# The recurrence of an RWKV-7 and pooling block on one core: a longer planned gap for the triangular inverse, the next pair but one begun earlier, and one table for exp and ln

## The chip, the core and the metric

The kernel runs on one core of a Trainium2 chip. A core has a matrix engine (TensorE, PE in the profile, with its weight loads as PEld), VectorE (DVE), ScalarE (ACT), GpSimd (POOL) and SyncE (SP), which here issues nearly all DMAs, in order, on one queue. Each engine runs its own instructions in a fixed order and waits on semaphores for the others. The metric is the device time of one execution in microseconds, the median of several; lower is better.

## The reference

One block of a decoder with 512 tokens and width 2048, in float32. A combined projection of the normalised input feeds two mixers: RWKV-7 heads (16 heads of 64) and causal pooling over windows of 2, 4, 8 and 16 tokens; then an output projection and a gated MLP with a short convolution.

```python
def _wkv7_scan(r, w, k, v, a, b):
    def step(S, inp):
        r_t, w_t, k_t, v_t, a_t, b_t = inp
        sa = jnp.einsum('bhvk,bhk->bhv', S, a_t)
        S = S * w_t[:, :, None, :] + sa[..., None] * b_t[:, :, None, :] + v_t[..., None] * k_t[:, :, None, :]
        y = jnp.einsum('bhvk,bhk->bhv', S, r_t)
        return S, y

def reference(x, c, ...):
    mod = c_act @ w_ada[l] + b_ada[l]
    h = _rmsnorm(x, norm1_g[l]) * (1.0 + sc1) + sh1
    p = h @ w_in[l]
    y_rwkv = _rwkv7_mixer(p[..., :N_RWKV_COLS], ...)
    y_pool = _pool_mixer(p[..., N_RWKV_COLS:], ...)
    x = x + gt1 * (jnp.concatenate([y_rwkv, y_pool], axis=-1) @ w_out[l])
    h = _rmsnorm(x, norm2_g[l]) * (1.0 + sc2) + sh2
    x = x + gt2 * _conv_ffn(h, w_up[l], conv_w[l], conv_b[l], w_down[l])
    return _rmsnorm(x, norm_f_g)
```

## The kernel before

**Stages.** The first 160 us stream adaLN weights and the first part of the input projection. The last stage, from 859 us on, is the output projection and the MLP. Between them lies the stretch that the change touches, the function `recurrence`, which interleaves four things on PE.

- *The rest of the input projection*: 27 output tiles of 128 columns, each 16 steps deep; each step is three matmuls of 512 columns (`mm3`, L122 to L124), since every float32 operand is split into a high and a low part. ACT casts the high part of the weights (`whi`, L115), DVE subtracts the low part (`wlo`, L117). `units` yields after each step, so three matmuls go together. Finished tiles are shifted and spilled to DRAM (`spill`, `sp`).
- *Part a of a head pair* (`stage_a`): decay and gate factors from small matmuls and sigmoids (L404 to L410), a scan, two exponentials (`ep`, `em`), the norm of k by ln and exp (`inv`, L432 to L434), then `ar` and `bt`. `scores` (L381) makes the 64x64 triangular matrices of eight chunks and two heads, masked into `sb` (L447).
- *The inverse of their 16x16 diagonal blocks*: the blocks go through DRAM (`dn`) into `nl`, one block per partition; 28 small DVE steps (L464 to L473) solve them; the result `xyl` goes through DRAM (`dxz`) into `x4w`, and ACT copies it to `x4` (L483).
- *Part b* (`stage_b`): scores of the other keys, four transposes into token rows (L502, copied by ACT, L503), from L530 on the 16-blocks are joined to 32 and 64 with small matmuls, then the chunk products, six scan steps over chunks (L601 on PE, L602 on DVE in turn), the output, and a normalisation and gate (L614 to L629).

Beside these, pool groups (L300) and the adaLN products (`ada_rest`, `war`, 192 tiles of 256 KB multiplied on DVE at L354) are spread over the stretch.

**What sets the order.** PE's order is written by hand: `recurrence` keeps a clock of planned microseconds. Each generator yields a pair (PE time of the step just issued, planned wait until its next step); the loop issues the first ready step of part b, part a or a pool group, and where none is ready a step of the projection. The inverse is planned as 27 us after the scores (`q.inverted`). A pair's part a starts when its projections are `made` and the pair two before has `left` its output. The order on ACT, DVE and SP isn't by hand: the scheduler of the framework sets it from priorities and its own estimate of times, and tiles with few buffers (`pa`: two PSUM banks; `ring`: seven; `x4c`, `ep`, `em`: one) hold a writer back until the readers are done.

```python
q.inverted = clock[0] + 27.0
...
if live["a"] is None and na < NP and na in made and (na < 2 or hasattr(qs[na - 2], "left")):
    live["a"], ready["a"] = stage_a(na, qs[na]), clock[0]
...
for c in "bap":
    if live[c] is not None and ready[c] <= clock[0]:
        break
```

Of the kernel before, what the change touches and what calls it, by code (L numbers as in the profile page):

```python
# [9 lines left out]
F32 = mybir.dt.float32  # L10
# [47 lines left out]
def block_kernel(ctx, tc, a, out, stop=None, dbg=None):  # L58
# [211 lines left out]
    def load_pw(gi):  # L270
        t = ra.tile([P, T], F32, tag="war", name="pw", bufs=3) if gi < 3 else ring("pw")
# [66 lines left out]
    dxz = [tc.dram_tile([32, 2, 32, 32], F32, name=f"dxz{i}") for i in range(2)]  # L338
    for i in range(2):
        nc.sync.dma_start(dxz[i][:, :, :, :].rearrange("l w i j -> (l w i j)").rearrange("(p n) -> p n", p=P),  # L340
                          x4w[:, :, :, 0:32])

# [29 lines left out]
    class Pair:  # L372
        pass
# [10 lines left out]
    def stage_a(p, q):  # L384
# [10 lines left out]
        lw = q.lw = ra.tile([P, 3, P], F32, tag="lw", name="lw", bufs=2)  # L395
        nc.sync.dma_start(lw, a["lora"][p, :, :, :])
# [7 lines left out]
        PE.matmul(psw, lw[0:64, 0, :], xwa[0:64, :], start=True, stop=True)  # L404
        PE.matmul(psal, lw[64:128, 0, :], xwa[64:128, :], start=True, stop=True)
# [4 lines left out]
        S.activation(al, psal, AF.Sigmoid, bias=col("a0", p))  # L410
        cs = ra.tile([P, NL, L + 1], F32, tag="sg", name="cs", bufs=2)
# [12 lines left out]
        yield 1.4, 2.0  # L424
# [4 lines left out]
        ar = q.ar = ra.tile([P, 2, NL, L], F32, tag="ar", name="ar", bufs=2)  # L429
        V.tensor_mul(ar[:, 1, :, :], ch(r), ep[:, :, 1 : L + 1])  # L430
# [5 lines left out]
        V.scalar_tensor_tensor(ar[:, 0, :, :], ch(inv), -1.0, ep[:, :, 0:L], op0=ALU.mult, op1=ALU.mult)  # L436
# [3 lines left out]
        yield 0.9, 13.0  # L440
# [9 lines left out]
        dn = tc.dram_tile([32, 32, 32], F32, name=f"dn{p}")  # L450
        for b in range(4):
            nc.sync.dma_start(dn[8 * b : 8 * b + 8, :, :].rearrange("s i j -> i s j"), nt[BS[b], :, half32(b)])
        nl = ra.tile([64, 16, 16], F32, tag="nl", name="nl")
        for e in range(2):
            es = slice(16 * e, 16 * e + 16)
            nc.sync.dma_start(nl[32 * e : 32 * e + 32, :, :], dn[0:32, es, es])
# [17 lines left out]
        dx = dxz[p % 2]  # L474
        for e in range(2):
            es = slice(16 * e, 16 * e + 16)
            for w in range(2):
                nc.sync.dma_start(dx[:, w, es, es], xyl[32 * e : 32 * e + 32, w, :, :])
        for b in range(4):
            nc.sync.dma_start(x4w[BS[b], :, :, half32(b)],  # L480
# [3 lines left out]
        q.inverted = clock[0] + 27.0  # L484
        yield 1.4, 6.0
# [19 lines left out]
    def stage_b(p, q):  # L505

        sb, x4, ar, bt, kt, v, fdec = q.sb, q.x4, q.ar, q.bt, q.kt, q.v, q.fdec
        nt = sb[:, :, 0, :]
# [10 lines left out]
        yield 1.4, 0.0  # L519
        to_rows(lambda c: v[:, c * P : (c + 1) * P], by_head(tok[:, 0, :, :]))  # L520
        to_rows(lambda c: ar[:, 0, 2 * c : 2 * c + 2, :].rearrange("p e t -> p (e t)"), by_head(rw[:, :, 0, :]))
        yield 0.9, 1.0
        to_rows(lambda c: bt[:, c * P : (c + 1) * P], by_head(sb[:, :, 2, :]))
        to_rows(lambda c: kt[:, c * P : (c + 1) * P], by_head(tok[:, 1, :, :]))
        yield 0.9, max(1.5, q.inverted - clock[0] - 0.9)
# [11 lines left out]
        yield 2.1, 1.6  # L537
# [6 lines left out]
        yield 2.1, 2.3  # L544
# [8 lines left out]
        yield 1.2, 1.6  # L553
# [3 lines left out]
        yield 1.2, 1.6  # L557
# [8 lines left out]
        yield 2.1, 1.6  # L566


        lo, hi = slice(0, NC * L), slice(NC * L, 2 * NC * L)
        first = {"start": False, "skip_group_check": True}  # L570
        pg = btile()
        for c, e, h, j, s in items:
            PE.matmul(pg[HS[h], e, jl(c)], rw[HS[e], s, 0, :], sb[HS[e], s, 2, :], start=c == 0, stop=True,
                      skip_group_check=True)
        for c, e, h, j, s in items:
            PE.matmul(pg[HS[h], e, jl(NC + c)], sb[HS[e], s, 2, :], rw[HS[e], s, 1, :], stop=False, **first)
        for c, e, h, j, s in items:
            PE.matmul(pg[HS[h], e, jl(NC + c)], tok[HS[e], 1, s, :], tok[HS[e], 0, s, :], stop=True, **first)
        py = btile("py")
        for c, e, h, j, s in items:  # L580
            PE.matmul(py[HS[h], e, jl(c)], rw[HS[e], s, 0, :], sb[HS[e], s, 1, :], start=c == 0, stop=True,
                      skip_group_check=True)
        for h in range(2):
            V.tensor_tensor(gd[HS[h], :, HS[h]].rearrange("p (c e) k -> p e c k", e=2),
                            pg[HS[h], :, lo].rearrange("p e (c k) -> p e c k", c=NC),
                            ident[HS[h], None, None, HS[h]].to_broadcast([64, 2, NC, L]), op=ALU.add)
        hs = rw[:, :, 0, :]
        V.tensor_tensor(hs.rearrange("p (c e) d -> p e c d", e=2), pg[:, :, hi].rearrange("p e (c d) -> p e c d", c=NC),
                        fdec[:, :, :].rearrange("p (c e) o -> p e c o", e=2).to_broadcast([P, 2, NC, L]), op=ALU.mult)
        for c, e, h, j, s in items:  # L590
            PE.matmul(py[HS[h], e, jl(NC + c)], rw[HS[e], s, 1, :], sb[HS[e], s, 1, :], stop=False, **first)
        for c, e, h, j, s in items:
            PE.matmul(py[HS[h], e, jl(NC + c)], tok[HS[e], 0, s, :], sk[HS[e], s, 1, :], stop=j == 0, **first)
# [739 lines left out]
```

## Time and profile before

| | us |
|---|---|
| median of 3 runs (lowest to highest) | 2441.68 (2439.91 to 2449.15) |
| the profiled execution | 2447.94 |
| its span, first to last instruction | 2446.0 |

PE is busy for 2217.8 us of the span (91%), PEld 1972.2, DVE 1620.6, ACT 1049.9. The mean granted TensorE clock is 0.964 of full speed.

How to read the rows that the prediction shows. A row of stretches gives the window and its length, then the busy time and number of instructions of PE, PEld, DVE, ACT and POOL, the granted clock, the share of the DMA engines and GB/s. A row of waits gives who waited for whom, the total in us, the number of times and the longest. A row in order of time gives start, length, engine, line, operation and tiles, and in brackets the idle time before it with what ended it; matmuls overlap, so the cost of one is the distance between starts. A row of groups has the count, the busy time, the mean in ns, and the idle time before them. A float32 matmul of the small kind stands as two rows of PE.

### The profile page before, as it was taken

What the parts mean: (1) busy time and instruction counts of PE and PEld (TensorE: products, weight loads), DVE (VectorE), ACT (ScalarE), POOL (GpSimd) and SP (SyncE); (2) the same over time, 40 slices, a digit from 0 to 9 for tenths busy, and PEclk for the clock granted to TensorE, in tenths of its full rate; (3) what the DMA queues carried; (4) which work ended last, traced back from release to release, by engine and by line L of the source; (5) the groups of instructions that cost most, each with busy time, mean ns of one, the idle gap of its engine ahead of it and who ended that gap; (6) DMA issues with size and microseconds to landing.
All of it is one profiled execution on the core that took longest, in us unless ns stands there. A gap on an engine that the chain in (4) does not pass through costs nothing.

```text
span 2446.0 us, 43166 instructions
## 1 busy us (share of the span) xinstructions
PE 2217.8 (91%) x17346; PEld 1972.2 (81%) x17346; DVE 1620.6 (66%) x2543; ACT 1049.9 (43%) x1447; POOL 126.3 (5%) x183
## 2 busy tenths in 40 slices
PE   4766866867888999999999999999999999999997
PEld 3645655655666779999999999999999988888897
DVE  7987776765446445678888887777777735353354
ACT  3232422424334334665555555555555622233353
POOL 0000000000000001001011010000000000110000
PEclk9988988889999999999999999999999999999998
DMA  9978667653433275669888887777777757764464
GB/s 352 336 229 231 184 196 205 188 152 101 96 77 77 80 249 184 182 212 261 241 240 237 237 233 199 198 200 201 196 197 194 256 166 277 255 195 129 112 182 162
DMA packets 226235, 482.89 MB, mean 197 GB/s; under 512 B 74545, under 2 KB 79729, under 8 KB 217841
## 3 DMA queue, kind: packets, MB, share of 16 engines
q1 hardware_dynamic: 206114, 413.01, 52.6%
q0 software_dynamic: 18864, 66.07, 13.2%
q8 instruction: 136, 2.23, 0.4%
q10 hardware_dynamic: 1056, 1.05, 0.1%
q14 instruction: 65, 0.53, 0.1%
HBM read 441.50 MB, written 38.54 MB: 196 GB/s over the span
## 4 chain that ended last, share of the span: by engine, by line
PE 48%; issue 8%; DVE 1%; DMA 1%; ACT 0%; POOL 0%; POOLq 0%; DVEq 0%; ACTq 0%
PE b L124 16%; PE b L123 16%; PE b L122 16%; DMA wrow<-wup 1%; DVE ulo L923 0%; DVE xr L851 0%; ACT x L854 0%; DVE t L977 0%; POOL x L1207 0%; ACT t L859 0%; ACT uhi L921 0%; DVE u L952 0%; DVE wlo L117 0%; DVE t L963 0%; DVE t L969 0%
## 5 line engine op out<-in xcount | busy, mean ns | idle before, releaser
L124 PE MATMUL b<-t,ulo 128*128 128x256 f32 x1408 | 397.2, 282 | 0.0
L122 PE MATMUL b<-t,uhi 128*128 128x256 f32 x1408 | 396.8, 282 | 0.0
L123 PE MATMUL b<-t,uhi 128*128 128x256 f32 x1408 | 396.7, 282 | 0.0
L124 PE MATMUL b<-act,ulo 128*128 128x512 f32 (+1 forms) x880 | 308.0, 350 | 0.0
L123 PE MATMUL b<-act,uhi 128*128 128x512 f32 (+1 forms) x880 | 307.8, 350 | 0.0
L122 PE MATMUL b<-act,uhi 128*128 128x512 f32 (+1 forms) x880 | 307.7, 350 | 0.0
L122 PE MATMUL b<-y,uhi 128*128 128x256 f32 x1056 | 297.4, 282 | 2.3 <-ACT uhi L921 2.3
L124 PE MATMUL b<-y,ulo 128*128 128x256 f32 x1056 | 297.3, 282 | 0.7 <-DVE ulo L923 0.6
L123 PE MATMUL b<-y,uhi 128*128 128x256 f32 x1056 | 297.1, 281 | 0.0
L115 ACT CAST whi<-wraw 128x512 fp32r<-128x512 f32 x236 | 145.4, 618 | 334.5 <-PE mm L123 198.9
L923 DVE TENSOR_TENSOR ulo<-wd,uhi 128x1024 fp32r<-128x1024 f32 (+1 forms) x120 | 136.2, 1136 | 214.6 <-ACT uhi L921 205.4
L122 PEld LDWEIGHTS b<-t,uhi 128*128 128x128 f32 x1408 | 266.9, 190 | 0.0
L124 PEld LDWEIGHTS b<-t,ulo 128*128 128x128 f32 x1408 | 266.9, 190 | 0.0
L123 PEld LDWEIGHTS b<-t,uhi 128*128 128x128 f32 x1408 | 266.8, 190 | 0.0
L921 ACT CAST uhi<-wquart 128x1024 fp32r<-128x1024 f32 x156 | 163.9, 1050 | 202.6 <-PE b L123 177.3
L921 ACT CAST uhi<-wd 128x1024 fp32r<-128x1024 f32 (+1 forms) x120 | 117.3, 978 | 290.5 <-PE b L123 289.4
L923 DVE TENSOR_TENSOR ulo<-wquart,uhi 128x1024 fp32r<-128x1024 f32 x156 | 190.9, 1225 | 71.6 <-ACT uhi L921 71.5
L117 DVE TENSOR_TENSOR wlo<-wraw,whi 128x512 fp32r<-128x512 f32 x236 | 161.4, 688 | 109.0 <-ACT whi L115 106.7
L122 PE MATMUL mm<-ah,whi 128*128 128x512 f32 x464 | 208.4, 449 | 5.5 <-ACT upad L267 5.5
L921 ACT CAST uhi<-r 128x1024 fp32r<-128x1024 f32 x132 | 138.7, 1050 | 163.1 <-PE b L123 158.0
L923 DVE TENSOR_TENSOR ulo<-r,uhi 128x1024 fp32r<-128x1024 f32 x132 | 161.3, 1222 | 61.5 <-ACT uhi L921 61.3
L122 PEld LDWEIGHTS b<-y,uhi 128*128 128x128 f32 x1056 | 199.6, 189 | 2.8 <-ACT uhi L921 2.7
(302 smaller groups left out, 4521.4 us busy)
## 6 DMA issues: line engine op xcount, KB each, us to landing
wquart<-wup SPq DMA_DIRECT2D x176, 512.0 KB, 4.8
wa<-ada SPq DMA_DIRECT2D x48, 1024.0 KB, 6.6
war<-ada SPq DMA_DIRECT2D x192, 256.0 KB, 3.6
wd<-wdn SPq DMA_DIRECT2D x80, 512.0 KB, 3.9
wraw<-win SPq DMA_DIRECT2D x140, 256.0 KB, 3.8
wraw<-wout SPq DMA_DIRECT2D x96, 256.0 KB, 3.5
wquart<-wup POOLq DMA_DIRECT2D x44, 512.0 KB, 7.4
r<-wup SPq DMA_DIRECT2D x44, 512.0 KB, 4.4
```

The source lines that it names most:

```text
L115: S.copy(hi, raw)
L117: eng.tensor_tensor(lo, raw, hi[:, :].bitcast(F32), op=ALU.subtract)
L122: PE.matmul(ps, wh, xh, start=start, stop=False, skip_group_check=more)
L123: PE.matmul(ps, wh, xl, start=False, stop=False, skip_group_check=more)
L124: return PE.matmul(ps, wl, xh, start=False, stop=stop, skip_group_check=more)
L921: S.copy(hi[:, 0:n], src)
L923: lo_of[0] = V.tensor_tensor(lo[:, 0:n], src, hi[:, 0:n].bitcast(F32), op=ALU.subtract)
```

## The change

Its parts:

- The inverse is planned at 44 us instead of 27, and the other planned waits of both parts become longer (scan steps 1.4 instead of 1.1, and so on). The projection yields after each single matmul.
- Part a of a pair starts when part b of the pair two before has *begun*, and its last factors (`ar`) and the scores wait until that pair has `left`. Pool groups start only after the first part a, and no part a starts while a pool group runs.
- The last part of part b (normalisation and gate) is a generator of its own, `post`, with the highest priority ("d"), and loads its gate weights itself.
- The diagonal blocks go through DRAM as 16x16 blocks: 8 stores and 1 load, then 1 store and 8 loads, instead of 4 and 2, then 4 and 4. Two DMAs that cleared `dxz` are gone.
- Two of the chunk products move ahead of the joining to 64, two others become one of 128 columns, and the results share other PSUM banks.
- After the two sigmoids of part a one activation table with both ln and exp is loaded, in program order.

```diff
-                mm3(ps, wh[:, sl], wl[:, sl], *H[k], start=k == 0, stop=k == KT - 1)
-                yield
+                xh, xl = H[k]
+                for i, (w, x) in enumerate(((wh, xh), (wh, xl), (wl, xh))):
+                    PE.matmul(ps, w[:, sl], x, start=k == 0 and i == 0, stop=k == KT - 1 and i == 2)
+                    yield
...
         S.activation(al, psal, AF.Sigmoid, bias=col("a0", p))
+        tc.keep_in_program_order(S.preload_act_table_set("natural_log_exp_and_others"))
...
-        yield 0.9, 13.0
+        yield 0.9, 11.0
+
+
+        while p > 1 and not hasattr(qs[p - 2], "left"):
+            yield 0.0, 0.5
+        ar = q.ar = ra.tile([P, 2, NL, L], F32, tag="ar", name="ar", bufs=2)
...
-        dn = tc.dram_tile([32, 32, 32], F32, name=f"dn{p}")
-        for b in range(4):
-            nc.sync.dma_start(dn[8 * b : 8 * b + 8, :, :].rearrange("s i j -> i s j"), nt[BS[b], :, half32(b)])
...
+        dn = tc.dram_tile([64, 16, 16], F32, name=f"dn{p}")
+        for b in range(8):
+            nc.sync.dma_start(dn[8 * b : 8 * b + 8, :, :].rearrange("s i j -> i s j"),
+                              nt[16 * b : 16 * b + 16, :, 16 * (b % 4) : 16 * (b % 4) + 16])
+        nc.sync.dma_start(nl, dn[:, :, :])
...
+        dx = tc.dram_tile([64, 2, 16, 16], F32, name=f"dx{p}")
+        nc.sync.dma_start(dx[:, :, :, :], xyl)
+        for b in range(8):
+            nc.sync.dma_start(x4w[16 * b : 16 * b + 16, :, :, 16 * (b % 4) : 16 * (b % 4) + 16],
...
-        q.inverted = clock[0] + 27.0
-        yield 1.4, 6.0
+        q.inverted = clock[0] + 44.0
+        yield 1.35, 6.0
...
+        py = btile("py")
+        more = {"start": False, "skip_group_check": True}
+        for c, e, h, j, s in items:
+            PE.matmul(py[HS[h], e, jl(c)], tok[HS[e], 1, s, :], tok[HS[e], 0, s, :], start=c == 0, stop=False,
+                      skip_group_check=True)
...
+            PE.matmul(pg[HS[h], e, c * 2 * L : (c + 1) * 2 * L], rw[HS[e], s, 0, :], sb[HS[e], s, 1:3, :], start=True,
+                      stop=True)
...
-            yield 0.25, 1.1
+            yield 0.25, 1.4
...
         q.left = True
-        yield 1.2, 1.2
...
+        q.post = post(p, q, py, y)
+        yield 1.2, 0.0
+
+    def post(p, q, py, y):
+
+        lg = ra.tile([P, 2, P], F32, tag="lg", name="lg")
+        nc.sync.dma_start(lg, a["lora"][p, :, 1:3, :])
+        yield 0.0, 1.5
...
-        yield 0.0, 9.0
+        yield 0.0, 15.0
...
-            if live["a"] is None and na < NP and na in made and (na < 2 or hasattr(qs[na - 2], "left")):
+            if live["a"] is None and na < NP and na in made and live["p"] is None and (na < 2 or qs[na - 2].begun):
...
-            for c in "bap":
+            for c in "dbap":
...
-                        clock[0] += 0.69
+                        clock[0] += 0.23
                         n += 1
-                        if n % 2 == 0:
+                        if n % 6 == 0:
```

**What moves on the engines.** Lines shift a little: in the changed kernel L378 is the scores (before L381), L401 and L402 the matmuls of the sigmoids (L404, L405), L405 and L407 the sigmoids, L426 the norm's matmul (L428), L488 the bonus (L489), L501 and L502 the transposes and their copies (L502, L503), L482 the copy of the inverse (L483), L619 and L624 the normalisation's matmuls (L614, L619), L333 a projection matmul. L530 to L542 and L601 to L606 keep their numbers.

PE, from the output of pair 1 (L606) on, before. The bonus of pair 2 stands here, since pair 2's scores came four scan steps earlier:

```order
L606 MATMUL py<-ar,rw 64x64 x14
L489 MATMUL pa<-k_2771,hmat 128x512
L122 MATMUL mm<-ah_697,whi 128x512
L123 MATMUL mm<-al_698,whi 128x512
L124 MATMUL mm<-ah_697,wlo 128x512
L614 MATMUL py<-y,hmat 128x512
L122 MATMUL mm<-ah_749,whi 128x512
L123 MATMUL mm<-al_750,whi 128x512
```

The same place now:

```order
L606 MATMUL py<-ar,rw 64x64 x14
L378 MATMUL pb<-ar,kt 64x128 x16
L501 MATMUL pa<-cmat,v 128x128 x4
L501 MATMUL pa<-cmat,ar 128x128 x4
L619 MATMUL py<-y,hmat 128x512
L426 MATMUL pa<-sq,hmat 128x512
L501 MATMUL pa<-cmat,bt 128x128 x4
L501 MATMUL pa<-cmat,kt 128x128 x4
L624 MATMUL py<-sqy,hmat 128x512
```

Part b of pair 2 (L378, L501) now begins at once after pair 1's output, and the norm of pair 3 (L426) stands in the middle of it; the scores of pair 2 lie back ahead of pair 1's own L530.

ACT around the copy of an inverse (`x` from `x4w`), before, pair 1. Here `rw` at L536 is the copy that the same pair needs next:

```order
L503 COPY tok<-pa 128x512
L115 CAST whi<-wraw 128x512
L483 COPY x_2080<-x4w 128x1024
L536 COPY rw<-pa 128x8x64
L115 CAST whi<-wraw 128x512
L235 ACTIVATE spill<-mm,drv 128x512
```

Now, pair 2:

```order
L115 CAST whi<-wraw 128x512
L482 COPY x_2615<-x4w 128x1024
L405 ACT_TABLE_LOAD
L405 ACTIVATE sg<-pa,vec 128x8x64
L407 ACTIVATE al<-pa,vec 128x512
L408 ACT_TABLE_LOAD
L608 COPY y<-py 128x2x4x64
L416 ACTIVATE ep<-cs 128x520
L418 ACTIVATE em<-cs 128x520
L115 CAST whi<-wraw 128x512
L502 COPY tok<-pa 128x512
```

Between the copy and anything of its own pair's part b now stand the sigmoids and exponentials of pair 3 and the output `y` of pair 1.

SP's queue from the stores of pair 1's blocks to the load `nl`, before:

```order
L452 DMA dn_2026<-sb 32x8x32 x4
L113 DMA wraw<-win 128x512
L353 DMA war<-ada 128x512 x2
L456 DMA nl<-dn_2026 32x16x16 x2
L113 DMA wraw<-win 128x512
```

and now:

```order
L456 DMA dn_2025<-sb 16x8x16 x8
L350 DMA war<-ada 128x512 x3
L458 DMA nl<-dn_2025 64x256
L113 DMA wraw<-win 128x512
L350 DMA war<-ada 128x512
```

There are twice the stores of half the rows, and one load instead of two; one more load of adaLN weights stands between.

More of the change, by code (lines that the diff above doesn't have):

```diff
@@ L337, in block_kernel @@
     G.memset(x4w, 0.0)
[L338 to L341, printed above, removed]
     cq = [None]
@@ L372, in block_kernel @@
     class Pair:
-        pass
+        begun = False
     items = [(c, e, h, 2 * c + e, 4 * h + c) for c in range(NC) for e in range(2) for h in range(2)]
@@ L543, in stage_b @@
         V.tensor_add(x4, x4, pX[:, :, :].rearrange("p w (s j) -> p s w j", s=8))
-        yield 2.1, 2.3
+        yield 2.2, 1.0
+        py = btile("py")
[3 more added lines that the diff above has]
+                      skip_group_check=True)
+        for c, e, h, j, s in items:
+            PE.matmul(py[HS[h], e, jl(NC + c)], tok[HS[e], 0, s, :], sk[HS[e], s, 1, :], stop=False, **more)
+        yield 1.25, 2.0
         pt = btile()
@@ L575, in stage_b @@
         for c, e, h, j, s in items:
-            PE.matmul(pg[HS[h], e, jl(NC + c)], sb[HS[e], s, 2, :], rw[HS[e], s, 1, :], stop=False, **first)
+            PE.matmul(py[HS[h], e, jl(c)], sb[HS[e], s, 2, :], rw[HS[e], s, 1, :], stop=True, **more)
         for c, e, h, j, s in items:
[L578 to L582, printed above, removed]
+            PE.matmul(py[HS[h], e, jl(NC + c)], rw[HS[e], s, 1, :], sb[HS[e], s, 1, :], stop=j == 0, **more)
@@ L589, in stage_b @@
+        V.tensor_tensor(hs.rearrange("p (c e) d -> p e c d", e=2),
+                        py[:, :, 0 : NC * L].rearrange("p e (c d) -> p e c d", c=NC),
                         fdec[:, :, :].rearrange("p (c e) o -> p e c o", e=2).to_broadcast([P, 2, NC, L]), op=ALU.mult)
[L590 to L593, printed above, removed]
@@ L625, in stage_b @@
         V.tensor_add(rs, rs, q.bv)
-        yield 0.9, 2.5
+        yield 0.9, 5.0
         pgt = py[:, 1, :]
-        PE.matmul(pgt, q.lw[:, 1, :], xg1, start=True, stop=False)
-        PE.matmul(pgt, q.lw[:, 2, :], xg2, start=False, stop=True)
+        PE.matmul(pgt, lg[:, 0, :], xg1, start=True, stop=False)
+        PE.matmul(pgt, lg[:, 1, :], xg2, start=False, stop=True)
         V.tensor_mul(rs, rs, pgt)
@@ L708, in recurrence @@
                     continue
-                waiting = [ready[c] for c in "bap" if live[c] is not None]
+                waiting = [ready[c] for c in "dbap" if live[c] is not None]
                 if not waiting:
@@ L716, in recurrence @@
             if step is None:
+                if c == "b":
+                    live["d"], ready["d"] = qs[nb].post, clock[0]
                 live[c] = None
```

68 lines of the change are left out of this document (28 added, 40 removed).

## The prediction

> **What bounds the kernel now.** I read the page first, then the stretches, then PE's waits inside one stretch, then one head pair's inverse in order of time.
>
> ```profile
> span 2446.0 us, 43166 instructions
> PE   4766866867888999999999999999999999999997
> PEclk9988988889999999999999999999999999999998
> ...
> 0.00:160.00 160.00, 102.63 (x394) 78.30 (x394) 133.97 (x195) 53.24 (x82) 2.75 (x11) 0.97 0.88 318
> 160.00:859.00 699.00, 549.80 (x5739) 418.68 (x5740) 436.32 (x1104) 250.90 (x357) 0.00 (x0) 0.90 0.52 147
> 859.00:2446.00 1587.00, 1565.33 (x11215) 1475.25 (x11213) 1050.34 (x1245) 745.72 (x1011) 123.59 (x172) 0.99 0.70 208
> ```
>
> The first 160 us carry 318 GB/s with the DMA engines 88% busy, and the change leaves them alone. The last 1587 us have PE busy for 1565. Only the stretch between, 160 to 859 us, holds the recurrence over the eight head pairs, and there PE stands still for some 150 of 699 us at a granted clock of 0.90. In the same row DVE is busy 436 us (62%), ACT 251, the DMA engines 52%: PE is the longest, but it is not fed. Its waits there, longest first (us in total, times, longest):
>
> ```profile
> PE pa L530 <- ACT x L483: 84.7, 8, 16.8
> PE pb L601 <- DVE rw L602: 16.5, 7, 4.0
> PE pa L300 <- DVE inv L432: 15.3, 1, 15.3
> PE py L628 <- DVE rs L623: 8.9, 7, 2.0
> PE mm L122 <- ACT upad L267: 5.5, 1, 5.5
> PE py L593 <- issue: 5.2, 3, 3.2
> PE pb L562 <- DVE sb L556: 4.6, 2, 3.4
> ...
> PE pa L502 <- DVE bv L491: 0.4, 1, 0.4
> ```
>
> All fourteen rows make 153.7 us. The first, once per pair, is the wait for the 16x16 inverse: PE's order is written by hand, and it reaches L530 before ScalarE has copied the inverse (L483). Pair 1 in order of time, PE, DVE, SP and ACT together:
>
> ```profile
> 276.86 1.03 PE L381 MATMUL pa<-ar,bt 64*64 64x128 f32 x29
> 281.43 1.28 DVE L447 TENSOR_TENSOR sb<-pa,masks 128x512 f32<-128x512 f32 x2
> 282.74 1.82 SPq L452 DMA_DIRECT2D dn<-sb  x4
> 286.43 0.86 SPq L456 DMA_DIRECT2D nl<-dn  x2
> ...
> 310.57 0.37 DVE L473 COPY xyl<-xyl 64x256 f32<-64x256 f32 x1
> 310.97 1.93 SPq L478 DMA_DIRECT2D dxz<-xyl  x4
> 314.55 1.92 SPq L480 DMA_DIRECT2D x4w<-dxz  x4
> 320.71 1.04 ACT L483 COPY x<-x4w 128x1024 f32<-128x1024 f32 x1 [12.48 <-DMA x4w<-dxz]
> 321.81 1.97 PE L530 MATMUL pa<-x,sb 64*64 64x64 f32 x32 [12.68 <-ACT x L483]
> ...
> 277.86:321.81 43.95, 28.53 (x178) 20.87 (x177) 31.81 (x103) 13.63 (x20) 0.00 (x0) 0.90 0.79 215
> 620.56:652.70 32.14, 25.54 (x139) 18.81 (x136) 16.22 (x45) 13.73 (x20) 0.00 (x0) 0.97 0.53 118
> ```
>
> From the end of the scores to L530 pass 43.95 us in pair 1 and 32.1 in pair 5 (the two window rows); PE has work for 28.5 and 25.5 of them. What lengthens pair 1 is DVE, busy 31.8 us in it against 16.2: the 28 small steps between L464 and L473 share DVE with the adaLN products, which are used up by pair 5.
>
> ```profile
> L354 DVE SCALAR_TENSOR_TENSOR war<-war,cq 128x512 f32<-128x512 f32 x192 | 130.4, 688 | 90.6 <-DMA war<-ada 88.7 <-DMA cq<-cact 1.2
> 308.27 0.40 PE L122 MATMUL mm<-ah,whi 128*128 128x512 f32 x1
> 308.50 0.39 PE L123 MATMUL mm<-al,whi 128*128 128x512 f32 x1
> ...
> 323.57 1.92 PE L533 MATMUL pa<-tok,sk 64*64 64x64 f32 x32
> 325.41 0.79 PE L122 MATMUL mm<-ah,whi 128*128 128x512 f32 x1
> 326.00 0.63 PE L123 MATMUL mm<-al,whi 128*128 128x512 f32 x1
> ...
> 328.19 1.15 PE L542 MATMUL pb<-Tm,x 64*64 64x64 f32 x32
> 329.17 1.10 PE L542 MATMUL pb<-x,Tm 64*64 64x64 f32 x32
> ```
>
> **The change, part by part.**
>
> *Inverse and cover.* From start to start a projection matmul takes 0.23 us (308.27, 308.50), a group of 16 small correction matmuls, two rows each, 0.98 (328.19, 329.17). Between scores and L530 the hand-written order held 96, 78, 69, 78, 72, 78, 69 and 78 projection matmuls in the eight pairs and now holds 143, 98, 104, 107, 125, 121, 102 and 95. For pair 5 that is 43 x 0.23 = 9.9 us more, and with six scan steps and three correction groups newly inside, some 15 us more, so about 40 us of work where there was 25.5; the other pairs come to 39 to 47 by the same count. Against that stands the inverse's length. Its four DMA legs stay four: 8 stores and 1 load for 4 and 2, then 1 store and 8 loads for 4 and 4. SP issued 4 in 1.82 to 1.93 us, so a leg of 8 takes 1.9 us longer to issue and a leg of one 0.5 to 1.5 us less; the two legs of 8 move half the bytes they did, which should give back the rest, and I take 0 (bounds -3 and +4 us a pair). What does change is DVE: the adaLN products are paced by projection matmuls, so with the same pacing and shorter stalls they reach to pair 6. DVE's new order has 8 to 10 of them inside the 28 steps of pairs 0 to 5 and 4 in pair 6, where it had 9 to 11 in pairs 0 to 3, 3 in pair 4 and none later. So I expect some 40, 48, 46, 45, 48, 43, 38 and 33 us for the eight inverses, with pair 1's 43.95 and pair 5's 32.1 as the rows to scale from. Less the cover of 40, 40, 47, 40, 40, 40, 40 and 39, some 24 us of waiting are left.
>
> *ACT's order.* Only PE's order is by hand; ACT and DVE are ordered by the scheduler. Before, the copy of the inverse was followed at once by what its own pair needs (L536). Now it stands ahead of the next-but-one pair's sigmoids, which hold the two PSUM buffers (pa) that PE's next transposes need. In pair 2 PE is stopped at L501, 4.4 us ahead of L530, and behind the copy wait a table load, two sigmoids, the copy of y and the exponentials. In pairs 0, 5 and 6 DVE's order likewise has the next pair's chain (inv, bt) ahead of L535, whose product L542 needs. A table load and an activation cost 1.28 and 0.6 to 0.7 us:
>
> ```profile
> L622 ACT ACT_TABLE_LOAD x8 | 10.3, 1283 | 0.1
> 624.14 0.69 ACT L621 ACTIVATE rs<-py,eps 128x512 f32<-128x512 f32 x1
> 624.84 1.28 ACT L622 ACT_TABLE_LOAD   x1
> 626.14 0.63 ACT L622 ACTIVATE rs<-rs 128x512 f32<-128x512 f32 x1
> ```
>
> Two loads and five activations are 6 us, DVE's four or five products at 0.7 another 3: 9 us after the copy, of which PE has 2 to 3 us of own work, so about 7 for each of those four pairs, 28 together (bounds 0, where the inverse is early, and 60, where all eight pay). With the 24 above, the 84.7 us become 52: **-33 us** (bounds -85 and 0).
>
> *Pool group.* Its four matmuls L300 now come 54 projection matmuls after the transposes instead of between the first pair's norm and scores, so the 15.3 us row goes: **-15** (bounds -15.3 and -5, since group 3's DVE work still has to go somewhere).
>
> *Post stage and tables.* 48 table loads in this stretch become 17. ACT is busy 251 of 699 us, so this is nothing by itself; what hides it is that slack, and if ACT were the bound it would be 31 x 1.28 = 40 us. But two of the loads per pair stand in the chain that PE's L628 waits for (8.9 us, and 1.6 in a row left out), and that step now has 5 us instead of 2.5 to hide in: **-8** (bounds -10.5 and 0).
>
> The Trainium skill ("ScalarE: Activation LUTs", section "What ACT_TABLE_LOAD costs") puts a drain of 1.38 us on top of each 1283 ns load. The rows show no such time: the activation ahead ends at 624.83, the load begins at 624.84 and the next activation at 626.14. By that figure the 31 loads would be 82 us of ACT and not 40, which would still lie in its slack.
>
> *Scan.* L601 gets 7 projection matmuls between steps instead of 6, 0.23 us more cover in 48 places, against a denser DVE: of 19.2 us (16.5, and 2.7 in a row left out) I let 14 stand, **-5** (bounds -12 and +8). `py` is taken earlier, ahead of L548; the product that frees it (0.7 us on DVE) is behind 3 to 9 us of PE work, so nothing, and 1 us a pair if it is late. Two correction groups move ahead of the solve, which costs nothing by itself, and two others merge into one of 128 columns: L381's form has it at 1.03 us, and at L542's 0.98 for each group replaced it could save up to 1 us a pair; I take nothing. The other rows (L122 5.5, L593, L562 and smaller) stay.
>
> *The clock.* After the 12.68 us wait L530 takes 1.76 us from start to start (321.81, 323.57) where the same number in L542 takes 0.98, and the projections behind it 0.59 and 0.43 instead of 0.23. Over eight pairs L530 and L533 lose 8 x (1.76 + 1.84 - 2 x 0.98) = 13 us; with the slow projections I put the loss near 28 us. Waits of 5 to 9 us will still bring some of it: **-10** (bounds -25 and 0).
>
> The Trainium skill ("TensorE: Matmul & The Clock Gate", section "What's actually happening") says that the clock halves after an idle window of about 3.4 us and returns after as long a busy one. By that rule, with waits that all fell under 3.4 us, the whole 28 us would come back and the sum would be 18 us lower. The slow rows behind the 12.68 us wait agree with it; no row here sets short waits apart.
>
> Sum: -33 - 15 - 8 - 5 - 10 = -71 us. The span of 2446 becomes 2375. The profiled execution took 2447.94 us, 1.9 more than its span, and the median of the three runs is 2441.68, 6.3 below that execution: I predict **2370 us**, 2.9% less.
>
> **Rivals.** (1) *The cover is long enough.* The inverses come in at the old 32 to 44 us, under 39 to 47, and the scheduler's place for the copy hardly matters: the inverse term is then -75 to -85, the clock -20 or more, and the time about 2325 (2300 to 2345). For it: DVE's work inside most pairs grew by 5 us or less. Against it: pair 1's 43.95 is already over its new cover of 40. (2) *The gain is spent at the copy.* All pairs pay the 9 us behind it, inverses average 46: the inverse term is -10, the clock nothing, and the time about 2405 to 2430. (3) *Slower.* ACT's queue, held by the copy, becomes the bound: the sigmoids, the exponentials and the weight casts of the projections stand behind the wait for the DMA, so PE runs dry of weights as well as of PSUM. Beside the four terms without the inverse (-38) it takes a wait of about (84.7 + 38 + 12)/8 = 17 us a pair to be slower by over 0.5%; with 9 us behind the copy, that is from an inverse of 48 us in every pair on. Only pairs 1 to 4 are near it. If it holds, 2455 to 2475. (4) That the change does not do what it says I rule out for PE, whose order shows the longer gaps; that ACT and DVE follow is what (2) and (3) doubt.
>
> **How the numbers follow.** Forecast (2345 to 2400) 0.50, rival 1 0.20, rival 2 0.19 (0.12 of it still faster by over 0.5%), rival 3 0.11. The lowest end, all terms at their best, is 2441.7 - 148 = about 2294; the highest with no gain at the inverse is 2425. From 2310 to 2425 holds about 0.8; the forecast's own range is 2345 to 2400. About 0.5% (12 us) is what a measurement of this kernel tells from no change: faster 0.82, within 0.07, slower 0.11.
>
> **What would show it.** Right: the wait of L530 for the copy falls to 15 to 40 us, and new PE waits for sigmoids or row copies (L405, L407, L502) and for Tm (L535) add 15 to 35; the L300 row is gone; the stretch from 160 us to the output projection lasts 610 to 645 us instead of 699, at a granted clock of 0.93 to 0.97; after it nothing changes by more than 5 us. Wrong: no new waits behind the copy (rival 1), or projections waiting for ACT's casts, which is none of the fourteen rows today (rival 3); or a gain outside this stretch.

## The result, and the profile after

| | before | after |
|---|---|---|
| median, us (lowest to highest, 4 runs each) | 2443.13 (2439.91 to 2449.15) | 2347.06 (2344.94 to 2349.00) |
| span of the profiled execution, us | 2446.0 | 2347.1 |
| mean granted TensorE clock | 0.964 | 0.981 |

The ratio is 0.9604, with a 95% interval of 0.9582 to 0.9626: 96 us, or 4.0%, were gained. The prediction was 2370 us in a range of 2310 to 2425.

The three stretches of the changed kernel:

```profile
0.00:160.00 160.00, 103.20 (x394) 78.66 (x394) 134.28 (x195) 52.79 (x81) 2.74 (x11) 0.97 0.87 317
160.00:761.05 601.05, 537.16 (x5480) 404.16 (x5481) 427.66 (x1105) 208.40 (x326) 0.00 (x0) 0.95 0.57 168
761.05:2347.00 1585.95, 1565.60 (x11217) 1475.65 (x11215) 1049.90 (x1245) 745.36 (x1011) 123.37 (x172) 0.99 0.70 208
```

The whole gain lies in the middle stretch: 699 us have become 601, while the first stretch and the last (1587.0, now 1586.0) are what they were. PE's busy time there fell by 13 us at a clock of 0.95 instead of 0.90; the rest of the gain is waiting that is gone. PE's waits in the stretch, largest first (us in total, times, longest):

```profile
PE pb L563 <- DVE Tm L560: 15.4, 4, 6.5
PE pb L601 <- DVE rw L602: 9.6, 10, 1.7
PE mm L333 <- DVE wlo L117: 8.1, 3, 4.7
PE pa L426 <- ACT sq L395: 8.0, 1, 8.0
PE mm L333 <- ACT upad L267: 7.1, 1, 7.1
PE pb L601 <- DVE rw L591: 3.7, 3, 2.2
PE pa L426 <- DVE Tm L535: 3.6, 2, 2.9
PE py L633 <- DVE rs L628: 2.6, 2, 1.7
...
PE pa L426 <- ACT tok L502: 2.0, 1, 2.0
PE pa L501 <- ACT sg L405: 1.6, 1, 1.6
PE pa L530 <- ACT sg L405: 1.6, 1, 1.6
```

All rows together make 67.8 us (153.7 before). The row that led the list, L530 for the copy of the inverse, isn't there at all. No row is left that stands once in every pair with ten microseconds in it; what leads now is `Tm`, a product on VectorE, late by up to 6.5 us.

Why L530 no longer waits: the elapsed time from the end of the scores to L530 in pairs 1 and 3, with the sum over all eight, and pair 3's copy in order of time.

```profile
265.68:318.80 53.12, 45.51 (x428) 33.41 (x423) 42.65 (x122) 19.89 (x30) 0.00 (x0) 0.94 0.61 180
386.91:440.60 53.69, 44.91 (x406) 33.82 (x400) 38.81 (x114) 16.06 (x26) 0.00 (x0) 0.94 0.64 191
sum 403.71, PE 358.56 PEld 264.26 DVE 289.84 ACT 150.36 POOL 0.00; mean PE 44.82 PEld 33.03 DVE 36.23 ACT 18.80 POOL 0.00
```

```profile
437.50 1.04 ACT L482 COPY x<-x4w 128x1024 f32<-128x1024 f32 x1
440.59 1.09 PE L530 MATMUL pa<-x,sb 64*64 64x64 f32 x30 [1.57 <-ACT sg L405]
```

In pair 3 the inverse is finished 51.6 us after the scores (386.91 to 438.54) and L530 comes 2 us later. Measured the same way, from the scores' end to the copy's end, the eight inverses take 41.1, 50.6, 42.7, 51.6, 42.3, 43.0, 39.0 and 31.6 us, 342 in sum. They did not become shorter: before, they took 313 us by the same measure, and four of them have grown by 5 to 11 us (pairs 1, 3, 5 and 6; pair 5 from 32.0 to 43.0). But they now lie under 404 us of elapsed time, their cover, where PE's arrival at L530 left them 229 before (314 us to L530 less its wait of 84.7).

### The profile page after: what moved, and what is told of

Same layout as the page of the kernel before. It is cut to its first block, busy times and chain, and to the rows that moved or that the text cites. A ratio compares the mean times of both kernels' runs of the same rounds, so it can differ in the third digit from the quotient of the medians.

```text
span 2347.1 us, 42629 instructions
## 1 busy us (share of the span) xinstructions
PE 2206.0 (94%) x17090; PEld 1958.5 (83%) x17090; DVE 1611.8 (69%) x2543; ACT 1006.5 (43%) x1416; POOL 126.1 (5%) x183
## 3 DMA queue, kind: packets, MB, share of 16 engines
q10 hardware_dynamic: 1056, 1.05, 0.1%
## 4 chain that ended last, share of the span: by engine, by line
PE 67%; DVE 12%; issue 11%; DMA 8%; ACT 2%; SPq 1%; POOL 0%; DVEq 0%; POOLq 0%; ACTq 0%
PE b L124 18%; PE b L122 18%; PE b L123 18%; PE mm L333 6%; DMA war<-ada 6%; DVE jk L214 3%; DVE war L351 2%; DVE wlo L117 1%; DMA wrow<-wup 1%; PE pa L300 1%; DVE sacc L199 0%; DVE al L151 0%; PE pb L570 0%; ACT ah L150 0%; DMA cq<-cact 0%
## 5 line engine op out<-in xcount | busy, mean ns | idle before, releaser
L124 PEld LDWEIGHTS b<-y,ulo 128*128 128x128 f32 x1056 | 200.1, 190 | 0.6 <-DVE ulo L932 0.6
```

Of the source, the lines that this page charges most:

```text
L124: return PE.matmul(ps, wl, xh, start=False, stop=stop, skip_group_check=more)
```

## The experiments

The theory: the gain is the longer gap, that is, more work of PE between the scores and L530. The rivals: the table loads, the smaller exchange, the earlier first part, or the single matmuls. Each kernel is the changed one with one edit, except where it says "before". Ratios are to the kernel before on the same chip, with 95% intervals; the change stands at 0.9604 (0.9582 to 0.9626). The runs come from several chips, so a difference of a few us between two of them is surer from the ratios, where 0.001 is 2.4 us.

**The gap, put back.**

```diff
-        q.inverted = clock[0] + 44.0
+        q.inverted = clock[0] + 27.0
```

> The changed kernel with one number put back: the planned time of the inverse is 27.0 again and not 44.0; single projection matmuls, one table, 16x16 blocks and the early first part stay. Theory (the gain is the longer planned gap, that is, more projection matmuls between the scores and the first matmul that needs the inverse): TensorE's waits for the copy of the inverse come back. The lengths of the inverse stay near 342 us in sum, the elapsed cover falls by about 15 us a pair from 404 us, so that 50 to 90 us of waiting stand at L530 and the time is 2400 to 2435 us. Rival 1 (fewer table loads and the smaller exchange shorten the inverse, and that is the gain): the gap hardly matters, 2345 to 2365 us. Rival 2 (the early first part makes the gain, by taking VectorE and ScalarE work out of the way): 2345 to 2375 us, with less than 25 us of waiting at L530.

2412.04 us, ratio 0.9877 (0.9857 to 0.9896): the theory's case in the time and in the wait at L530. Its first row of PE's waits, in the same view:

```profile
PE pa L530 <- ACT x L482: 79.8, 8, 15.7
```

One number brings back the row almost whole (84.7 before) and 65 of the 96 us. The other 31 us, from before to here, go with other rows of that view: L300's 15.3 us and the post stage's 10.5 are gone, L601's 19.2 is 11.9, while L563's wait for `Tm` rises from 0.9 to 9.8.

Two steps of the expectation failed and made up for each other. The inverses did not stay near 342 us but took 300, and the elapsed time up to PE's arrival at L530 fell by 23 us a pair, from 404 us to 220, and not by 15. By this count, inverses of 342 us would have left some 120 us of waiting. The inverse grows with the gap, at least in part because the adaLN products on VectorE are paced by the projection matmuls: 92 of them fall between the scores and the copy here, 124 in the changed kernel.

**The gap alone, in the kernel before.**

```diff
-        q.inverted = clock[0] + 27.0
+        q.inverted = clock[0] + 34.0
```

> The kernel before with one number changed: the planned time of the inverse is 34.0 and not 27.0; projection matmuls still go in threes, tables, exchange blocks and the start of the first part are the old ones. Theory (the gap is the gain): the cover of each of the 8 pairs grows by some 6 to 7 us, the 84.7 us of waiting for the inverse fall by 35 to 55 us, time 2388 to 2410 us. Rival (a longer gap does nothing without the shorter exchange or the earlier first part, since the inverse's length grows along with it or other waits take its place): 2430 to 2450 us.

2385.66 us, ratio 0.9764 (0.9748 to 0.9780), 57 us, 2 us better than the theory's bounds.

```profile
PE pa L530 <- ACT x L483: 25.4, 4, 8.3
PE pa L300 <- DVE inv L432: 15.5, 1, 15.5
```

Seven planned microseconds in eight pairs are 56 us, and 57 came, without any other part of the change. The wait at L530 fell by 59 us, while the pool group's 15 us stayed. That the sum comes to seven a pair is luck: by pair the wait fell by 1.4 to 16.9 us. Pairs 2 and 5, before and then here:

```profile
409.44 1.97 PE L530 MATMUL pa<-x,sb 64*64 64x64 f32 x32 [16.85 <-ACT x L483]
652.70 1.98 PE L530 MATMUL pa<-x,sb 64*64 64x64 f32 x32 [5.74 <-ACT x L483]
...
378.80 1.15 PE L530 MATMUL pa<-x,sb 64*64 64x64 f32 x32
612.41 1.97 PE L530 MATMUL pa<-x,sb 64*64 64x64 f32 x32 [4.34 <-ACT x L483]
```

In four pairs the wait is gone, and the inverses have grown here too, from 313 us in sum to 339 (pair 5: 32.0 to 45.2).

**The gap in between.** 36.0 instead of 44.0.

> The changed kernel with the planned time of the inverse at 36.0 and not 44.0. Theory (a gap is worth what it lacks against the length of the inverse, pair by pair): the slack between the copy and its use was 11.4, 2.6, 14.4, 2.1, 4.1, 5.5, 10.9 and 11.0 us; with 8 us less, four pairs come short by 5.4, 5.9, 3.9 and 2.5 us, so some 18 us of waiting at L530 and 2355 to 2372 us. Rival 1 (the gap is worth its full length in every pair): 64 us more, 2395 us or later. Rival 2 (the inverse gets shorter along with its cover, since fewer fillers bring less work on VectorE): 2340 to 2352 us.

2355.22 us, ratio 0.9653 (0.9637 to 0.9669), at the theory's lower end.

```profile
PE pa L530 <- ACT x L482: 17.6, 6, 5.4
PE pb L601 <- DVE rw L602: 17.3, 7, 4.0
PE pb L563 <- DVE Tm L560: 8.6, 5, 2.8
```

The waiting at L530 came out as counted (18 expected, 17.6), but it cost only 8 us (12 by the ratios), since other rows gave way to it (L563: 15.4, now 8.6): all rows make 69.7 us, against 68.0. From 27 to 36 a microsecond of gap brought 6.3 us (56.8 / 9), from 36 to 44 only 1.0 to 1.5. At 36 six of the eight pairs still wait, at 44 none does. The length to be covered isn't fixed, though: the inverses take 300, 328 and 342 us in sum at 27, 36 and 44, so rival 2 was right about the inverse, and a part of each longer gap goes to the inverse itself.

**One table, taken away.**

```diff
-        tc.keep_in_program_order(S.preload_act_table_set("natural_log_exp_and_others"))
```

> The changed kernel without the one line that loads the table which holds both exp and ln: 48 table loads in the stretch of the recurrence, as before, and not 17. Theory (the gap is the gain): 31 loads of 1.28 us each fall on ScalarE, which is busy for less than half of the time; a few stand in a chain (sigmoid to exp, ln to exp, the copy behind them), so 2350 to 2365 us, 3 to 18 us slower than the change, and the waits at L530 hardly grow. Rival (the table loads were the gain): 2390 to 2440 us. A loss of 25 to 40 us would say that both count.

2361.87 us, ratio 0.9664 (0.9643 to 0.9684), 15 us later, inside the theory's bounds. L530 waits no longer for the copy; the loss stands in chains of ScalarE and VectorE:

```profile
PE pb L600 <- DVE rw L601: 11.5, 9, 3.3
...
PE py L632 <- DVE rs L627: 6.0, 3, 4.5
PE pb L541 <- DVE Tm L534: 5.7, 3, 2.8
```

All of its PE waits sum to 82.8 us against 68.0 (both to 865 us), which is the whole loss. The table is worth about 15 us on top of the gap, and not the gap's 65. If the parts add up, that is about half of the 31 us that the gap doesn't account for; the rest (the stage `post` with its longer planned waits, the rules for pool groups, the products of 128 columns) wasn't tried part by part.

**The first part, put back.**

```diff
-... live["p"] is None and (na < 2 or qs[na - 2].begun):
+... live["p"] is None and (na < 2 or hasattr(qs[na - 2], "left")):
```

> The changed kernel with the old rule for the first part: it starts only when the state of the pair two before has been left, and no longer when that pair's second part has begun. The gap stays 44.0. Theory (the gap is the gain, the early start only keeps the first part out of the way of the inverse): 2347 to 2385 us; the waits at L530 for the copy stay below 20 us, and what is lost stands at the norms, the scores and the ends of the first part, which now falls behind the planned gap. Rival (the early first part is what makes room for the gap): 2400 to 2440 us, most of what was gained goes.

2349.47 us, ratio 0.9614 (0.9597 to 0.9631): not to be told from the change. Beginning the first part earlier moved instructions, and no time that can be told from none.

**The exchange, put back.** Stores and loads of the inverse through 32x32 blocks, as before.

> The changed kernel with the old exchange of the inverse: 4 and 2 transfers out and 4 and 4 back through 32x32 blocks in memory, in place of 8 and 1 and 1 and 8 through 16x16 blocks. The gap stays 44.0. Theory (the gap is the gain, the exchange's form is not): the legs of the exchange stay within 1 us a pair, the slack between the copy and its use (2.1 to 14.4 us) covers what they lose, 2343 to 2357 us. Rival (the smaller exchange was a real part of the gain, through shorter legs or less traffic for the weight loads): 2362 to 2395 us, with waits at L530 in the pairs whose slack was 2 us.

2337.47 us, ratio 0.9571 (0.9551 to 0.9592): below both expectations, 10 us better than the change (8 by the ratios), though the two intervals overlap slightly. The smaller exchange was no part of the gain. Nor is the old one shorter: the inverses take 350 us here, against 342. What else gained isn't shown; one thing that differs is the order. ScalarE's copy stands at another place in its queue; in pair 0 it begins at 237.82 us, behind a later pair's sigmoids and exponentials and with no idle time, and PE's norm waits 2.1 us instead of 8.0:

```profile
237.82 1.03 ACT L490 COPY x<-x4w 128x1024 f32<-128x1024 f32 x1
```

**Threes again.** The projection yields after three matmuls, planned as 0.69 us.

> The changed kernel with projection matmuls between the steps in threes again (0.69 us of planned time each, one product of the adaLN part for every two threes) and not one at a time. Theory (the gap is the gain): planned waits are rounded up to 0.69 and not to 0.23 us, so steps go at most half a microsecond later each and the fillers last no longer: 2340 to 2362 us. Rival (the single matmuls are a main part, by bringing the recurrence's steps forward): 2370 to 2400 us.

2339.68 us, ratio 0.9579 (0.9559 to 0.9600), just under the theory's bounds; the single matmuls aren't where the gain is.

**The copy on GpSimd.**

```diff
-        S.copy(x4, x4w)
+        G.tensor_copy(x4, x4w)
```

> The changed kernel with the copy of the inverse on GpSimd and not on ScalarE, so that no instruction of ScalarE is queued behind the wait for the transfers. Theory of the head of the line (pair 0: the copy held ScalarE for 6.1 us and TensorE's norms of the next pair waited 8.0 us for the squares): that wait goes to below 1 us and the time falls to 2336 to 2343 us, as long as the slower copy fits the slack of 2.1 to 14.4 us. Rival 1 (the time saved at the norms is lost again at the next step of the same chain, or the copy is late for its use in the two pairs with 2 us of slack): 2344 to 2352 us. Rival 2 (the copy on GpSimd takes VectorE's way to the memory or is slow, several us): 2353 us or more, with waits at L530 for GpSimd.

2342.51 us, ratio 0.9594 (0.9572 to 0.9616): not to be told from the change, although the median lies just inside the theory's bounds. The wait that was to vanish, L426 for the squares, is 6.6 us and not below 1. ScalarE in pair 0, with the copy in its queue (the change) and without (here):

```profile
237.06 1.04 ACT L482 COPY x<-x4w 128x1024 f32<-128x1024 f32 x1 [6.12 <-DMA x4w<-dx]
238.13 1.28 ACT L416 ACT_TABLE_LOAD   x1
239.42 0.64 ACT L416 ACTIVATE ep<-cs 128x520 f32<-128x520 f32 x1
239.96 0.70 ACT L395 ACTIVATE sq<-rkv,vec 128x512 f32<-128x512 f32 x1
```

```profile
230.74 1.28 ACT L416 ACT_TABLE_LOAD   x1
237.73 0.64 ACT L416 ACTIVATE ep<-cs 128x520 f32<-128x520 f32 x1 [5.71 <-DVE cs L414]
238.27 0.71 ACT L395 ACTIVATE sq<-rkv,vec 128x512 f32<-128x512 f32 x1
```

With the copy out of the way ScalarE stands for 5.71 us at the next instruction, for VectorE's `cs`. And VectorE stood behind the adaLN products, which wait for their weights (the changed kernel, just ahead of that scan):

```profile
230.07 0.69 DVE L351 SCALAR_TENSOR_TENSOR war<-war,cq 128x512 f32<-128x512 f32 x1 [1.84 <-DMA war<-ada]
...
232.49 0.69 DVE L351 SCALAR_TENSOR_TENSOR war<-war,cq 128x512 f32<-128x512 f32 x1 [1.72 <-DMA war<-ada]
...
235.85 1.23 DVE L410 TENSOR_TENSOR_SCAN cs<-scanm,sg 128x520 f32<-128x520 f32 x1
```

The scan's input was ready at 230.44 (L405: 229.75 and 0.69), and it began 5.4 us later. So the wait that looked like the copy's has two causes that end at nearly the same time, and taking away one leaves the other. The next three runs go to the second.

**Two buffers for the adaLN vector.**

```diff
-                cq[0] = ra.tile([P, T], F32, tag="cq", name="cq")
+                cq[0] = ra.tile([P, T], F32, tag="cq", name="cq", bufs=2)
```

> The changed kernel with two buffers for the vector that the adaLN products take (four loads in the stretch), so that VectorE need not stand behind its load; the room comes from leaving out a small copy of the middle column (8 instructions on VectorE, the same result). Theory (VectorE, held by transfers at the head of its queue, is what is left of the waits: 6.5 us at L563 in one pair, and wlo): these waits fall by 4 to 10 us, 2337 to 2343 us. Rival (the products behind are held by their weights anyway, 3.6 us for the next tile): 2344 to 2349 us, no change.

2342.29 us, ratio 0.9584 (0.9567 to 0.9600): inside the theory's bounds, with the row of `Tm` (L563 in the change) at 10.1 us, but not to be told from the change. The edit also leaves out the small copy named above.

**Four buffers for the adaLN weights.** `bufs=4` instead of 3 for `war` and for the pool weights that share its buffers; the small copy is left out here too.

> The changed kernel with four buffers and not three for the weights of the adaLN products; the room comes from leaving out the small copy of the middle column (8 instructions on VectorE, the same result). Theory (VectorE stands 81 us behind these loads in the stretch, and one buffer more lets a load be issued one product, about 1.4 us, earlier): VectorE's wait for them falls below 60 us, TensorE's waits by 4 to 12 us, 2334 to 2343 us. Rival (the loads are late because the DMA queues are, and a buffer more only moves the wait): VectorE's wait stays at 70 us or more, 2343 to 2350 us.

2336.61 us, ratio 0.9580 (0.9564 to 0.9596): inside the theory's bounds, 10 us better than the change (6 by the ratios), its interval overlapping the change's. PE's waits fell from 68.0 us to 58.6. What the small copy alone is worth wasn't tried; the run before, without it too, came out 5 us better than the change, which is within the noise. VectorE's wait for these loads, in the view of its own waits, the change first, then this kernel:

```profile
DVE war L351 <- DMA war<-ada: 73.7, 61, 3.7
...
DVE war L351 <- DMA cq<-cact: 6.7, 3, 4.0
```

```profile
DVE war L351 <- DMA war<-ada: 53.7, 40, 5.8
```

Another 8.5 us ahead of these products stand there in a row "issue", for which the profile shows no releaser, so the fall may be smaller than 20 us.

**No adaLN products at all.**

> The changed kernel without the 192 adaLN products and their loads in the stretch (left out altogether, so that VectorE has 130 us less to do there and never stands behind such a load). Theory (what is left of TensorE's waits in the stretch comes from VectorE held at the head of its queue by these loads): the waits at L563, at the norms and for wlo fall from 32 us to below 12 us, the time to 2310 to 2328 us, and the inverse gets 6 to 10 us shorter a pair where products stood in it. Rival (the waits that are left are chains of the recurrence itself, PE to VectorE and back): 2330 to 2345 us, with the rows of L563 and L601 as they are.

2279.56 us, ratio 0.9338 (0.9324 to 0.9352), 67 us less than the change and below the theory's 2310. The first two rows of PE's waits, and the stretch:

```profile
PE mm L333 <- ACT upad L267: 5.5, 1, 5.5
PE pb L602 <- DVE rw L603: 4.2, 6, 1.1
```

```profile
160.00:690.00 530.00, 517.21 (x5466) 392.41 (x5467) 317.72 (x714) 204.28 (x321) 0.00 (x0) 0.99 0.33 93
```

The waits sum to 19.9 us, within the stretch the rows of `Tm`, squares and `wlo` are at 0.7 us or gone, and the clock is 0.99. The inverse takes 30.5 to 33.6 us in every pair, 255 in sum against 342: 0.7 us less for each of the 124 products that lay inside, about the time of one (0.69). This run takes away VectorE's work, its waits for the loads and the loads' traffic together; of the three, only the waits were tried without the others, and only in part (four buffers).

**Three edits together**: the old exchange, threes, and four buffers.

> The changed kernel with three edits together that each took time off alone: the old exchange of the inverse (2337 us), projection matmuls in threes (2340 us), and four buffers for the weights of the adaLN products (2337 us). Theory (each removes its own waits): the gains of 10, 7 and 10 us add up at least in part, 2318 to 2332 us. Rival (all three only shift the order on VectorE and ScalarE around the same 192 products, whose work is unchanged): no better than the best of them, 2333 to 2345 us. In both cases it is below 2345 us and so ahead of the change and of the kernel before.

2323.62 us, ratio 0.9523 (0.9510 to 0.9536; 5 runs): the theory's case, the three gains add up for the most part, and the interval lies clear of the change's. PE's waits sum to 48.6 us, VectorE's for its adaLN loads to 44.4 (34.1 and 10.3). This is the fastest kernel of the study that computes everything.

## Why the prediction was right, and where its sizes were off

The direction, the place and the mechanism, a longer gap over the inverse, were right; one term of the sum was too small by half, and another was left at nothing. By the rows of PE's waits, before and after:

| term | forecast, us | measured, us |
|---|---|---|
| inverse and what stands behind its copy | 84.7 to 52: -33 | 84.7 to 19.3: -65 |
| pool group (L300) | -15 | 15.3 to 0: -15 |
| post stage | -8 | 10.5 to 2.6: -8 |
| scan (L601) | -5 | 19.2 to 13.3: -6 |
| clock and the rest of PE's work | -10 | -13 |
| other rows | 0 | 24.0 to 32.6: +9 |
| span | -71 | -99 |

The 19.3 us are the rows of L426, L501 and L530, which wait for sigmoids, row copies, `Tm`, the norm's factor and the squares; none of them waits for the copy itself. The clock's term is what the span's 98.9 us leave beside 85.9 us of waiting.

Of the signs that were named, L300's lost row, the clock of 0.95 (0.93 to 0.97) and the unchanged rest came. The stretch of 601 us (610 to 645), the wait at L530 (none, where 15 to 40 was forecast) and the new rows behind the copy (10 us by kind, where 15 to 35 was forecast) did not. The time lies just inside the narrower range of 2345 to 2400 only because the two misses, -65 for -33 and +9 for nothing, have opposite signs; that is luck.

*Inverse and cover.* The lengths were forecast well: 341 us in sum, measured 342, and within 7 us in each pair. The step that failed is the cover, "40, 40, 47, 40, 40, 40, 40 and 39". PE was busy for 44.8 us a pair in the same interval and not for 41, and 45 us in all were its other waits inside it, which lengthen the cover as well: 404 us elapsed in place of 326. With PE's work alone pairs 1 and 3 would have come short by 5 and 7 us; the waits inside closed that, so of the 24 us forecast none was left. The run at 36 shows the same from the other side: 17.6 us at L530 cost 8. PE's own work was 4 us a pair longer than counted. It isn't the projection: the trace has the counted number of its matmuls in seven intervals, and one less (142) in pair 0. In part it is the clock, but not all: pairs 4 and 7 ran at 1.00 and had 42.7 and 41.7 us of work where 40 and 39 were counted, so some 2.7 us are small matmuls of the recurrence that were counted too short or left out.

```profile
467.96:514.40 46.44, 42.70 (x329) 31.62 (x325) 35.16 (x106) 16.98 (x26) 0.00 (x0) 1.00 0.69 202
662.20:704.80 42.60, 41.65 (x395) 30.95 (x390) 25.90 (x70) 14.18 (x23) 0.00 (x0) 1.00 0.29 72
```

*ACT's order.* 28 us were expected behind the copy in four pairs. The kind of rows came, sigmoids, row copies and `Tm` at 10 us in all (15 to 35 forecast), and in pair 0 the norm, 8.0 us for the squares. But even that one isn't the copy's alone: on GpSimd it left 6.6 of the 8.0, with VectorE held by the adaLN loads. Elsewhere the copy found its data there, or nearly, as in pair 3: ScalarE stood idle ahead of the eight copies for 8.5 us in all (74.3 before), 6.1 of them in pair 0, and the copies ended 2 to 14 us before their use.

*Pool, post, scan* came as forecast. All the kernels built on the change have lost the pool's row (0.4 us at most), also with the old start of the first part; in the kernel before with the longer gap it stayed. Which of the other new rules for pool groups does it wasn't tried. For tables the forecast named ScalarE's slack as the cover; whether it hides them in the kernel before wasn't tried. After the gap, 31 more loads cost 15 us, and the rows that grew there are chains of ScalarE and VectorE.

*Other rows*, left unchanged in the sum, grew by 9 us: `Tm` for L563 from 0.9 to 15.4, `wlo` from nothing to 8.1. The largest, 6.5 us, is VectorE behind the load of the adaLN vector (4.01), with its queue already late from a load of weights (3.64):

```profile
386.97 0.69 DVE L351 SCALAR_TENSOR_TENSOR war<-war,cq 128x512 f32<-128x512 f32 x1 [3.64 <-DMA war<-ada]
...
393.84 0.69 DVE L351 SCALAR_TENSOR_TENSOR war<-war,cq 128x512 f32<-128x512 f32 x1 [4.01 <-DMA cq<-cact]
...
395.68 0.68 DVE L560 TENSOR_TENSOR Tm<-pb,mlev 128x512 f32<-128x512 f32 x1
```

*The rivals.* The first, a cover that is long enough, is what came of the inverse: its wait at L530 is gone. It was right for another reason than its own, though, which had inverses of 32 to 44 us under 39 to 47 of work: they took 31.6 to 51.6 us under 42.6 to 57.2 of elapsed time. Its 2325 was also mis-added: its terms (-75 to -85, -15, -8, -5 and -20 from 2441.7) give 2309 to 2319, and the range's upper end of 2425 comes to 2414 by the middle values of pool, post and scan, or to 2445 with every term at its worst. Rival 1's time wasn't reached because 19 us of waiting stand where the inverse's stood, the other rows grew by 9, and the clock's term was 13. The second and third, the gain spent at the copy or ScalarE as the bound, found no row in the changed kernel: projections wait 8.1 us for VectorE's low parts, and none for ScalarE's casts.

## What to carry to other kernels

Where an order is planned by hand, compare each planned gap with the measured length of what it covers, one item at a time: in these runs a microsecond of gap over eight items brought 6 to 8 us while most items were still waited for, and 1.0 to 1.5 from 36 us on. Count as cover what passes, other waits included, and not only the engine's work, and measure the covered length anew, since work that is paced by the cover can lengthen it. Once the large wait is gone, look for an engine that stands behind a load at the head of its queue: here leaving out the adaLN products, with their loads, took off 67 us more. What they cost in the kernel before, beyond the longer inverses of its first five pairs, wasn't tried.

## What the runs showed of the hardware

The granted clock follows the waits closely. In the stretch it was 0.90 with 154 us of PE waiting, 0.95 with 68 and 0.99 with 20, so waiting goes with a cost beyond its own time: without the adaLN products PE's waits fell by 48 us and the kernel by 67, and PE's busy time in the stretch fell by 20 us (537.2 to 517.2) for nearly as many instructions (5480 and 5466). The Trainium skill ("TensorE: Matmul & The Clock Gate", section "What's actually happening") lets the clock fall after idle windows of about 3.4 us; the traces agree only in part. In the changed kernel every wait of 4.2 us and more is followed by projection matmuls 0.42 to 0.59 us apart, where they are 0.23 apart otherwise. But one of 2.17 us is followed by such rows too, while before one of 3.32 us isn't; the changed kernel first, then the kernel before:

```profile
531.49 1.82 PE L563 MATMUL pb<-x,Tm 64*64 64x64 f32 x32 [2.17 <-DVE Tm L560]
533.24 0.79 PE L333 MATMUL mm<-ah,whi 128*128 128x512 f32 x1
533.83 0.63 PE L333 MATMUL mm<-al,whi 128*128 128x512 f32 x1
...
539.86 0.43 PE L601 MATMUL pb<-rw,gd 128*128 128x64 f32 x2 [3.32 <-DVE rw L602]
...
540.42 0.40 PE L123 MATMUL mm<-al,whi 128*128 128x512 f32 x1
540.66 0.40 PE L124 MATMUL mm<-ah,wlo 128*128 128x512 f32 x1
```

So the length of one wait alone doesn't tell whether the matmuls behind it are slow.

GpSimd copied the 128x1024 float32 tile in 1.04 to 1.29 us (eight copies, five of them 1.04), where ScalarE took 1.04 to 1.05; I had reckoned with a slower copy.
